# Sums of weights in the buffer of their quarters, a third raw tile, and second-half attention pieces at double distances

## The chip, the cores and the metric

One core of a Trainium2 chip runs the whole program: a two-layer decoder trunk in float32. Its engines are TensorE (PE, matmuls; PEld is its weight load), VectorE (DVE), ScalarE (ACT), GpSimd (POOL) and SyncE (SP), which issues most DMAs. Each engine works through its own list of instructions in order; semaphores order the engines among one another. The metric is the device time of one execution in microseconds (us); lower is better.

## The reference

x is 256 tokens by 2048 channels, d_ff is 8192. Each of the two layers computes

```python
h = rmsnorm(x, attn_norm_g[l])
q, k, v, gate_b, gate_c, conv_in = split(h @ w_in[l])          # six parts of 1024 columns
attn = diff_attention(rmsnorm(q), rmsnorm(k), v, lam, rel_bias)  # 8 heads, two softmaxes each
attn = rmsnorm(attn, subln_g[l]) * (1 - lam_init)
conv = gate_b * short_conv(gate_c * conv_in, conv_w[l])
x = x + concat([attn, conv]) @ w_out[l]
hm = rmsnorm(x, mlp_norm_g[l]) @ w_up[l]
x = x + square(relu(hm)) @ w_down[l]
```

## The kernel before

**Two parts of every operand.** A float32 matrix product is made of three matmuls with operands split in a high part (ACT copies and rounds it) and a low part (DVE subtracts the high part from the original). The three terms are high by high, high activation by low weight, low activation by high weight, in this order. So each weight tile costs DMA, one ACT instruction and one DVE instruction before PE can use it; `whi`, `wlo`, `uhi`, `ulo` and the parts named below are such tiles. Weights come from HBM once; the tiles `raw` (512 KB), `uraw` and `draw` (1 MB each) hold them as they arrive.

**What sets the order.** PE's instructions stand in the order in which the program writes them. Those of the other engines are placed at build time by a scheduler which plans with the dependencies and its own costs; instructions handed to `late` keep their program order. `Background.tick()`, called from the matmul loops, advances generators: a generator that yields n goes on n ticks later. So attention's pieces lie between the projection matmuls.

**Mixer.** Per layer the projections run in the order q, k, v for heads 0 to 3, q, k, v for heads 4 to 7, then (gate_C, conv_in) four times, gate_B four times, and the output projection `o`. `linear_t` makes the gate and convolution parts (`gc`, `ci`, `gb`, line 408), each with four "turned" raw tiles. `attention(..., pace)` is started twice per layer, with pace 1 for the first four heads and pace 2 for the last four. It takes four `unit`s (heads), each with scores (`sc`, line 604), softmax, then after a yield the transposes (`ptp`, line 635) and their parts `pT` (637, 638), after another yield the product with v (`av`, line 648), and after the last head the normalised `an` (668), a yield, and the transposes into `cat` (682). `staggered` starts the units a given number of ticks apart. The MLP's tiles take the room of the mixer's once these are read; the first four `uraw` loads (line 809) wait for that. SP issues them in its order among the mixer's raw loads (line 343).

**MLP.** The hidden units come in 32 pairs of blocks (index i). For each i PE makes two columns of hm (`upw`, `upc`, line 949, from `uhi`/`ulo`), ACT and DVE square them (`h`), make the four sums of activations S1 to S4, and split them into `f` (981 high, 982 low). Two pairs later (LAG = 2) the product of `f` with rows of w_down follows for the first half of w_down's columns, in a seven-product scheme instead of eight block products: product 1 takes the quarter b11 of the 2 x 2 blocks of weights, 2 takes b21, 3 takes b22, 5 and 7 take the sums t1 and t3, 6 and 4 take t2 and t4. In the MLP's first stage the products 1, 2, 3, 5 run between the two columns of pair i, the products 7, 6, 4 after the second. The second half of w_down's columns follows after the first stage: blocks `ordinary` (eight products, line 1074), and for the nine pairs in `SEVEN = (2, 4, 7, 9, 12, 14, 17, 19, 22)` the seven-product scheme in one run of 21 matmuls in the order 1, 2, 3, 5, 7, 6, 4. The activations of these pairs come back from HBM (`fb`, `back`).

**The weights of the scheme.** `quarters(i, col)` makes them in three steps. `plain` loads a `draw` tile (line 826; pool `dpool`, two buffers) and makes the parts of b11 (`b1h`, `b1l`, 512 elements per partition) and of b21, b22 (`b2h`, `b2l`, 1024 elements). `sums` makes t1, t3 in a tile `t` of 8 KB per partition (line 853, 1024 elements), their parts `t13h`, `t13l`, and then t2 (856) and t4 (857), 512 elements each. `more` makes the parts `t24h`, `t24l` of t2 and t4. All parts come from the helper lines 839 (ACT) and 840 (DVE). The `t13` and `t24` parts have one buffer each, `b1` and `b2` two.

Of the kernel before, what the change touches and what calls it, by code (L numbers as in the profile page):

```python
# [9 lines left out]
F32 = mybir.dt.float32  # L10
# [5 lines left out]
P = 128  # L16
# [12 lines left out]
CH = 512  # L29
# [59 lines left out]
def staggered(pieces, apart):  # L89

    entries = [[i * apart, p] for i, p in enumerate(pieces)]
    while entries:
        for e in list(entries):
            if e[0] <= 0:
                try:
                    e[0] = max(1, next(e[1]))
                except StopIteration:
                    entries.remove(e)
                    continue
            e[0] -= 1  # L100
        if entries:
            yield 1
# [3 lines left out]
def trunk(ctx: ExitStack, tc: tile.TileContext, x, w_in, w_out, conv_w, q_norm_g, k_norm_g,  # L106
          lambda_q1, lambda_k1, lambda_q2, lambda_k2, subln_g, attn_norm_g, mlp_norm_g,
          w_up, w_down, rel_bias, selector, out):
    nc = tc.nc
# [16 lines left out]
    def bank(name):  # L126
        return ps.tile([P, CH], F32, tag="bank", name=name)
# [456 lines left out]
    def attention(l, qT, kT, kL, v, h0, dst, bias, tmp, pace):  # L584
# [3 lines left out]
        parts = dst.open()  # L588
# [5 lines left out]
        def unit(i):  # L594
            h = h0 + i
# [30 lines left out]
            for t in range(NT):  # L626
# [2 lines left out]
                                               nlam[:, l:l + 1], op0=ALU.mult, op1=ALU.mult)  # L629
                nc.vector.scalar_tensor_tensor(p[:, w], s[:, 1, w], c[:, t:t + 1], s[:, 0, w],  # L630
                                               op0=ALU.mult, op1=ALU.add)
            yield 10
            tp = bank(f"ptp{h}")
            for b in range(3):
                nc.tensor.transpose(tp[:, b * P:(b + 1) * P], p[:, b * P:(b + 1) * P], ident)
            pT = tmp.tile([P, 2, 3 * P], F32R, tag="pT", name=f"pT{h}", bufs=1)
            nc.scalar.activation(pT[:, 0], tp[:, :3 * P], AF.Copy)
            nc.vector.tensor_sub(pT[:, 1], tp[:, :3 * P], pT[:, 0].bitcast(F32))
            yield 4

            av = ps.tile([P, CH], F32, tag="av", name=f"av{h}", bufs=1)
            av = av.rearrange("p (t n c) -> p t n c", t=NT, n=2)
# [23 lines left out]
            for t in range(NT):  # L666
# [3 lines left out]
                    ao[:, t].rearrange("p (g d) -> p g d", d=P),  # L670
                    f2[:, :, t:t + 1].to_broadcast([P, 4, P]), op=ALU.mult)
                an_.append(an)
            yield 12 if pace == 1 else 18
            for t in range(NT):
                tp = bank(f"atp{h0}_{t}")
                for b in range(4):
# [7 lines left out]
                    op0=ALU.mult, op1=ALU.subtract)  # L684
                yield 2

        yield from staggered([unit(i) for i in range(4)], 8)
        dst.ready = True

    def conv(l, q, u, cv, norm):  # L690
# [25 lines left out]
    def mixer(l, norm, loads):  # L716

        with ExitStack() as scope:
# [28 lines left out]
            for half in range(2):  # L747
                h0 = 4 * half
                acc = linear(f"q{l}{half}", hT, weights)
                r = norm.r  # L750
                qT = bpool.tile([P, 2, 4, S], F32R, tag="b", name=f"qT{l}{half}")
                work.start(qk_norm(acc, r, q_parts(qT), q_gain[:, l:l + 1], f"q{l}{half}"))
                acc = linear(f"k{l}{half}", hT, weights)
                kT = bpool.tile([P, 2, 4, S], F32R, tag="b", name=f"kT{l}{half}")
                work.start(qk_norm(acc, r, k_parts(kT, kL), k_gain[:, l:l + 1], f"k{l}{half}"))
                acc = linear(f"v{l}{half}", hT, weights)
                v = bpool.tile([P, 2, NT, CH], F32R, tag="b", name=f"v{l}{half}")
                for t in range(NT):
                    nc.scalar.activation(v[:, 0, t], acc[:, t], AF.Copy, scale=r[:, t:t + 1])
                    nc.vector.scalar_tensor_tensor(v[:, 1, t], acc[:, t], r[:, t:t + 1],  # L760
                                                   v[:, 0, t].bitcast(F32),
                                                   op0=ALU.mult, op1=ALU.subtract)
                work.start(attention(l, qT, kT, kL, v, h0, cat[half], bias, tmp,
                                     1 + half), 3 + 6 * half)
# [25 lines left out]
    def mlp(l, mnorm, last):  # L790
# [3 lines left out]
        with ExitStack() as scope:  # L794
            upool = scope.enter_context(tc.tile_pool(name="upool", bufs=4))
            fpool = scope.enter_context(tc.tile_pool(name="fpool", bufs=2))
            dpool = scope.enter_context(tc.tile_pool(name="dpool", bufs=2))
            spool = scope.enter_context(tc.tile_pool(name="spool", bufs=1))
            work.start(mnorm.factors(), 1)

# [2 lines left out]
            raws, forms = {}, {}  # L803
# [20 lines left out]
            def load_rows(i, col, pool=dpool, tag="draw"):  # L824
                raw = pool.tile([P, 2, 2 * CH], F32, tag=tag, name=tag)
                nc.sync.dma_start(
                    raw, w_down[l][i * 2 * P:(i + 1) * 2 * P, col:col + 2 * CH].rearrange(
                        "(k p) c -> p k c", p=P))
                return raw

            def quarters(i, col=0):


                keep = late if i == 0 or (i == SEVEN[0] and col) else lambda ins: None

                def parts(src, tag, bufs):
                    hi = spool.tile(list(src.shape), F32R, tag=f"{tag}h", name=f"{tag}h", bufs=bufs)
                    lo = spool.tile(list(src.shape), F32R, tag=f"{tag}l", name=f"{tag}l", bufs=bufs)
                    keep(nc.scalar.activation(hi, src, AF.Copy))  # L839
                    keep(nc.vector.tensor_sub(lo, src, hi.bitcast(F32)))  # L840
                    return hi, lo

                def plain():
                    raw = forms["raw"] = load_rows(i, col).rearrange("p k (n c) -> p k n c", n=2)
                    h1, l1 = parts(raw[:, 0, 0], "b1", 2)
                    h2, l2 = parts(raw[:, 1], "b2", 2)
                    return (h1, l1), (h2[:, 0], l2[:, 0]), (h2[:, 1], l2[:, 1])

                def sums():
                    raw = forms["raw"]  # L850
                    t = forms["t"] = spool.tile([P, 4, CH], F32, tag="t", name="t")

                    keep(nc.vector.tensor_sub(t[:, 0:2], raw[:, :, 1], raw[:, 0]))  # L853
                    h, lw = parts(t[:, 0:2], "t13", 1)

                    keep(nc.vector.tensor_add(t[:, 2], t[:, 1], raw[:, 0, 0]))
                    keep(nc.vector.tensor_sub(t[:, 3], raw[:, 1, 0], t[:, 2]))
                    return (h[:, 0], lw[:, 0]), (h[:, 1], lw[:, 1])

                def more():  # L860
                    h, lw = parts(forms["t"][:, 2:4], "t24", 1)
                    return (h[:, 0], lw[:, 0]), (h[:, 1], lw[:, 1])

                if (i, col) == (0, 0):
                    made = {}
                    forms["plain"] = lambda: made.update(p=plain())
                    forms["sums"] = lambda: made.update(s=sums())
                    return lambda: made["p"], lambda: made["s"], more
                return plain, sums, more

            def rows(i, k, box, col=0, *where):
# [124 lines left out]
            for i in range(NP):  # L996
                j = i - LAG
                end = i == NP - 1
                h = fpool.tile([P, 8, P], F32, tag="h", name="h", bufs=1)
# [12 lines left out]
                for c in range(2):  # L1012
# [24 lines left out]
                    elif j >= 0:  # L1037
                        t2, t4 = weights.take()
# [113 lines left out]
            for i in range(2 * BLK):  # L1152
# [14 lines left out]
                t2, t4 = weights.take()  # L1167
# [40 lines left out]
    for l in range(DEPTH):  # L1208
        mnorm = mixer(l, norm, first_loads if l == 0 else lambda weights: None)
        norm = mlp(l, mnorm, l == DEPTH - 1)  # L1210
# [31 lines left out]
```

## Time and profile before

| | |
|---|---|
| median of 3 runs | 2151.07 us (2148.47 to 2151.32) |
| the profiled execution | 2151.32 us, span 2149.5 us |
| PE busy | 2134.0 us (99%), 10934 matmuls |
| DVE busy | 1678.6 us (78%) |
| ACT busy | 1308.2 us (61%) |
| POOL busy | 169.8 us (8%) |
| HBM | 440.52 MB read, 33.58 MB written, 221 GB/s over the span |
| granted PE clock | 1.00 |

Times of single instructions are counted from the start of the span. A row of the timeline gives start, duration, engine, line, operation, tiles and shape; in brackets stands how long the engine was idle before, and what ended that. Where a row stands for several instructions it carries their number (x8) and the time from the first one's start to the last one's end. Neighbouring matmuls, ACT and DVE instructions overlap a little, so the distance between starts is shorter than a duration.

### The profile page before, as it was taken

The page shows a single profiled execution, that of the slowest core. Times are in us where ns is not written, and L with a number is a line of the kernel's source. Part 1 is how long each engine was busy: PE and PEld are TensorE (multiplying, and loading weights), DVE is VectorE, ACT ScalarE, POOL GpSimd, SP SyncE. Part 2 cuts the span into 40 slices and gives each one's busy share as a digit, 9 for nine tenths or more (in the row PEclk, how much of TensorE's full clock was granted, in tenths as well). Part 3 has the DMA queues.
Part 4 walks back from the last instruction along what each step waited for, and adds up shares of the span by engine and source line. Part 5 has one row for each costly group of instructions (what it writes and reads, how often), then busy time and mean ns, then how long its engine had stood idle before and what let it go on. Part 6 is the DMA issues. An engine that isn't in the chain of part 4 may idle for free. (4 is left out here: it accounts for less than half of the span.)

```text
span 2149.5 us, 28983 instructions
## 1 busy us (share of the span) xinstructions
PE 2134.0 (99%) x10934; PEld 1819.9 (85%) x10934; DVE 1678.6 (78%) x2297; ACT 1308.2 (61%) x1767; POOL 169.8 (8%) x226
## 2 busy tenths in 40 slices
PE   9999999999999999999999999999999999999999
PEld 8888888888888888888888888888888888888887
DVE  6777655799889888798566776557888888888984
ACT  6666445666666666565566654446666666665652
POOL 3111100000000000011110111000000000001110
PEclk9999999999999999999999999999999999999999
DMA  8555766577777777798665566656777777777984
GB/s 271 179 160 171 246 186 187 190 244 230 233 232 231 229 227 234 241 318 288 210 178 176 166 197 215 187 176 204 241 233 223 240 229 226 235 225 262 335 264 137
DMA packets 298524, 475.98 MB, mean 221 GB/s; under 512 B 10803, under 2 KB 191621, under 8 KB 298384
## 3 DMA queue, kind: packets, MB, share of 16 engines
q1 hardware_dynamic: 268768, 406.88, 60.4%
q0 software_dynamic: 29568, 67.24, 9.4%
q8 instruction: 85, 1.39, 0.3%
q14 instruction: 55, 0.45, 0.1%
q10 hardware_dynamic: 48, 0.02, 0.0%
HBM read 440.52 MB, written 33.58 MB: 221 GB/s over the span
## 5 line engine op out<-in xcount | busy, mean ns | idle before, releaser
L303 DVE TENSOR_TENSOR wlo<-raw,whi 128x1024 fp32r<-128x1024 f32 x286 | 352.2, 1234 | 252.3 <-ACT whi L302 245.8
L302 ACT ACTIVATE whi<-raw 128x1024 fp32r<-128x1024 f32 x286 | 303.1, 1060 | 341.1 <-PE o L386 73.6
L949 PE MATMUL upc<-nT,uhi 128*128 128x512 f32 x1920 | 477.7, 391 | 0.6 <-ACT ev L959 0.6
L816 ACT ACTIVATE uhi<-uraw 128x1024 fp32r<-128x1024 f32 x256 | 271.2, 1060 | 280.3 <-PE upc L949 260.4
L949 PEld LDWEIGHTS upc<-nT,uhi 128*128 128x128 f32 x1920 | 352.7, 188 | 69.2 <-ACT ev L959 1.1
L817 DVE TENSOR_TENSOR ulo<-uraw,uhi 128x1024 fp32r<-128x1024 f32 x256 | 312.9, 1223 | 109.3 <-ACT uhi L816 105.3
L949 PEld LDWEIGHTS upc<-nT,ulo 128*128 128x128 f32 x1920 | 261.9, 190 | 18.7
L949 PE MATMUL upc<-nT,ulo 128*128 128x256 f32 x1920 | 267.7, 282 | 0.0
L386 PE MATMUL o<-whi,cat 128*128 128x512 f32 x512 | 159.5, 390 | 0.0
L1074 PE MATMUL dn<-whi,fb 128*128 128x512 f32 x480 | 151.1, 389 | 0.0
L386 PEld LDWEIGHTS o<-whi,cat 128*128 128x128 f32 x512 | 96.1, 188 | 19.7
L302 ACT ACTIVATE whi<-uraw 128x1024 fp32r<-128x1024 f32 x60 | 63.7, 1061 | 75.7 <-PE dn L1074 70.7
L1074 PEld LDWEIGHTS dn<-whi,fb 128*128 128x128 f32 x480 | 90.1, 188 | 18.7
L386 PE MATMUL o<-wlo,cat 128*128 128x512 f32 x256 | 99.6, 389 | 0.0
L840 DVE TENSOR_TENSOR t13l<-t,t13h 128x1024 fp32r<-128x1024 f32 x78 | 95.5, 1224 | 4.0 <-ACT t13h L839 2.2
L839 ACT ACTIVATE b2h<-draw 128x1024 fp32r<-128x1024 f32 x78 | 82.5, 1058 | 24.9 <-PE pr L992 22.2
L840 DVE TENSOR_TENSOR b2l<-draw,b2h 128x1024 fp32r<-128x1024 f32 x78 | 95.5, 1224 | 2.1 <-ACT b2h L839 2.1
L840 DVE TENSOR_TENSOR t24l<-t,t24h 128x1024 fp32r<-128x1024 f32 x78 | 95.2, 1221 | 1.4 <-ACT t24h L839 0.3
L853 DVE TENSOR_TENSOR t<-draw 128x1024 f32<-128x1024 f32 x78 | 95.3, 1221 | 0.4
L992 PE MATMUL pr<-t13h,f 128*128 128x512 f32 x240 | 93.8, 391 | 0.0
L1074 PE MATMUL dn<-wlo,fb 128*128 128x512 f32 x240 | 93.4, 389 | 0.0
L303 DVE TENSOR_TENSOR wlo<-uraw,whi 128x1024 fp32r<-128x1024 f32 x60 | 73.2, 1224 | 21.1 <-ACT whi L302 20.9
(408 smaller groups left out, 4138.6 us busy)
## 6 DMA issues: line engine op xcount, KB each, us to landing
uraw<-in_w_up_dram SPq DMA_DIRECT2D x128, 1024.0 KB, 6.5
raw<-in_w_in_dram SPq DMA_DIRECT2D x191, 512.0 KB, 4.0
draw<-in_w_down_dram SPq DMA_DIRECT2D x82, 1024.0 KB, 5.3
raw<-in_w_out_dram SPq DMA_DIRECT2D x64, 512.0 KB, 3.6
uraw<-in_w_down_dram SPq DMA_DIRECT2D x30, 1024.0 KB, 6.3
raw<-in_w_down_dram SPq DMA_DIRECT2D x16, 1024.0 KB, 5.2
hid0p<-f POOLq DMA_DIRECT2D x21, 512.0 KB, 6.4
fb<-hid0p POOLq DMA_DIRECT2D x21, 512.0 KB, 5.9
```

What stands on the lines that cost most here:

```text
L302: pair = (nc.scalar.activation(hi, raw, AF.Copy), nc.vector.tensor_sub(lo, raw, hi.bitcast(F32)))
L303: nc.vector.tensor_sub(lo, raw, hi.bitcast(F32)))
L386: nc.tensor.matmul(acc[:, t], a.ap[:, pa, k % KG, t * P:(t + 1) * P], (hi, lo)[pw][:, j], start=(k == 0 and n == 0), stop=(k == nk - 1 and ...
L816: pair = (nc.scalar.activation(hi, src, AF.Copy), nc.vector.tensor_sub(lo, src, hi.bitcast(F32)))
L817: nc.vector.tensor_sub(lo, src, hi.bitcast(F32)))
L839: keep(nc.scalar.activation(hi, src, AF.Copy))
L840: keep(nc.vector.tensor_sub(lo, src, hi.bitcast(F32)))
L853: keep(nc.vector.tensor_sub(t[:, 0:2], raw[:, :, 1], raw[:, 0]))
L949: nc.tensor.matmul(acc[:, 0] if part else acc, wt[:, k], a.ap[:, 0, k % KG] if part else a.ap[:, :, k % KG], start=(part == 0 and kh == 0 ...
L992: nc.tensor.matmul(prods[n], f[:, pa, a], b[pw], start=(start and m == 0), stop=(stop and m == 2))
L1074: nc.tensor.matmul(prods[p], f[:, pa, 2 * k + t], b[pw][:, n], start=(p in starts and k == 0 and m == 0), stop=(stop and k == 1 and m == 2))
```

## The change

It has two parts. In `attention` every distance is multiplied by `pace`: the first four heads keep theirs (10, 4, 12 ticks and 8 between units), the last four get 20, 8, 24 and 16 instead of 10, 4, 18 and 8.

In `quarters` the tile `t` goes away. The sums are written over the quarters they are made of: t3 over b22 and t1 over b12 (in this order, by reversed views, since t3 reads b12 too), t2 over b11 and t4 over b21. `dpool` gets a third buffer of 8 KB per partition, which is the room that `t` had. The first sum therefore follows the `b1` and `b2` parts of the same tile, and a `draw` tile is free for the next load after its `t24l` instead of after its t4. The number of instructions on each engine and their shapes stay the same; lines behind the sums move down by two (853 becomes 854, 856 becomes 858, 857 becomes 859, 982 becomes 984, 1074 becomes 1076).

```diff
-            yield 10
+            yield 10 * pace
...
-            yield 4
+            yield 4 * pace
...
-            yield 12 if pace == 1 else 18
+            yield 12 * pace
...
-        yield from staggered([unit(i) for i in range(4)], 8)
+        yield from staggered([unit(i) for i in range(4)], 8 * pace)
...
-            dpool = scope.enter_context(tc.tile_pool(name="dpool", bufs=2))
+            dpool = scope.enter_context(tc.tile_pool(name="dpool", bufs=3))
...
                 def sums():
                     raw = forms["raw"]
-                    t = forms["t"] = spool.tile([P, 4, CH], F32, tag="t", name="t")
-                    keep(nc.vector.tensor_sub(t[:, 0:2], raw[:, :, 1], raw[:, 0]))
-                    h, lw = parts(t[:, 0:2], "t13", 1)
-                    keep(nc.vector.tensor_add(t[:, 2], t[:, 1], raw[:, 0, 0]))
-                    keep(nc.vector.tensor_sub(t[:, 3], raw[:, 1, 0], t[:, 2]))
+                    t31 = raw[:, ::-1, 1]
+                    keep(nc.vector.tensor_sub(t31, t31, raw[:, 0, ::-1]))
+                    h, lw = parts(raw[:, :, 1], "t13", 1)
+                    t2, t4 = raw[:, 0, 0], raw[:, 1, 0]
+                    keep(nc.vector.tensor_add(t2, raw[:, 1, 1], t2))
+                    keep(nc.vector.tensor_sub(t4, t4, t2))
                     return (h[:, 0], lw[:, 0]), (h[:, 1], lw[:, 1])
 
                 def more():
-                    h, lw = parts(forms["t"][:, 2:4], "t24", 1)
+                    h, lw = parts(forms["raw"][:, :, 0], "t24", 1)
                     return (h[:, 0], lw[:, 0]), (h[:, 1], lw[:, 1])
```

## The prediction

> **What bounds the kernel now.** I read the page's busy times first, then PE's waits, then the timeline around each of these, and last the order in which the changed kernel's instructions stand on each engine.
>
> ```profile
> PE 2134.0 (99%) x10934; PEld 1819.9 (85%) x10934; DVE 1678.6 (78%) x2297; ACT 1308.2 (61%) x1767; POOL 169.8 (8%) x226
> ```
> ```profile
> PE pr L992 <- DVE f L982: 3.1, 2, 1.7
> PE ci L408 <- ACT whi L302: 1.9, 2, 1.6
> PE ptp L635 <- DVE s L630: 1.7, 2, 0.8
> PE sc L604 <- DVE cat L682: 1.2, 2, 0.6
> PE warm L160 <- DVE mhalf L152: 1.1, 1, 1.1
> PE av L648 <- DVE pT L638: 1.0, 2, 0.5
> PE upc L949 <- ACT ev L959: 0.6, 1, 0.6
> ```
>
> PE is the bound: 2134.0 of 2149.5 us, and no matmul is added or removed. The second view gives us in total, times and the longest for all that PE waited for: 10.6 us, about one of each per layer. So at most about 10 us (0.5%) can be gained, and the loss is open: the sums are made anyway, but where they stand on DVE and ACT decides whether PE waits. The profiled execution took 2151.32 us (1.8 around the span), 0.25 above the median; sums are made against it. No change that this kernel's measurement can tell is 0.2%, or 4.3 us.
>
> **1. Second-half attention at double distances: -4.6.** By the changed kernel's order, `sc` stays where it is (1.2 stay). `ptp` of each later head comes 20 ticks after its scores and `av` 8 ticks after `ptp`, twice as far; ten and four more ticks of projection matmuls then cover what was late by 0.5 to 0.8 us. So 1.7 and 1.0 go. `ci` waited for a raw tile:
>
> ```profile
> 1206.83 66.08 SPq L343 DMA_DIRECT2D raw<-in_w_in_dram  x20
> 1273.99 7.39 SPq L809 DMA_DIRECT2D uraw<-in_w_up_dram  x4
> 1281.48 13.30 SPq L343 DMA_DIRECT2D raw<-in_w_in_dram  x5
> ```
> ```profile
> 1292.08 1.06 ACT L302 ACTIVATE whi<-raw 128x1024 fp32r<-128x1024 f32 x1 [7.80 <-DMA raw<-in_w_in_dram]
> ```
>
> SP stood at the four `uraw` loads until attention's last tiles were free, issued 4 MB in a row, and the next raw tile came behind them: 1292.08 - 1273.99 = 18.1 us for 4.5 MB. The changed order has three `uraw`, one raw, the fourth `uraw`, ten raw tiles later than before, when the tiles are long free. Three `uraw` and a raw take 3.5/4.5 of 18.1 = 14.1 us, and ACT could do with 18.1 - 1.6 = 16.5; the raw behind the fourth has 5 MB before it lands, 20.1 us against 16.5 and one raw tile's distance (66.08/20 = 3.3), 19.8. So `ci`'s 1.9 go, with 0 to 0.3 per layer given back; I take 0. Sum: 1.7 + 1.0 + 1.9 = 4.6. The cover of the remaining waits is PE's projection work, which is the same.
>
> **2. A third raw tile removes the stall late in the product stage: -3.7.** In layer 1:
>
> ```profile
> 1507.24 10.11 SPq L809 DMA_DIRECT2D uraw<-in_w_up_dram  x2
> 1517.59 0.40 SPq L826 DMA_DIRECT2D draw<-in_w_down_dram  x1
> ```
> ```profile
> 1528.79 0.63 ACT L839 ACTIVATE b1h<-draw 128x512 fp32r<-128x512 f32 x1 [5.29 <-DMA draw<-in_w_down_dram]
> 1533.32 2.11 PE L949 MATMUL upc<-nT,uhi 128*128 128x512 f32 x8 [0.65 <-ACT ev L959]
> 1541.29 0.50 PE L992 MATMUL pr<-b1h,f 128*128 128x512 f32 x1 [1.66 <-DVE f L982]
> ```
>
> With two tiles the load waited for t4 of two pairs back, went out behind two `uraw` loads, and ACT could use it 11.2 us after its issue; ACT stood 5.29 us with `ev`, `f` and all else queued behind `b1h`. After, three loads go out at the stage's start and each later one waits for `t24l` of three pairs back, a whole pair earlier than needed. So PE's 3.1 (`pr`) and 0.6 (`upc`) go.
>
> The Trainium skill, "Perfetto Trace Analysis", section Identifying Performance Opportunities, says that the same gap repeating on the engine that should be saturated can mean too little SBUF for the next tile. The `b1h` row agrees, and by that rule alone the buffer would be a plain gain of these 3.7 us; the next two points are what it does not count.
>
> **3. The first sums of each layer stand ahead of the first product: +8.0.** Before, `f` of pair 0 was done long before the first product:
>
> ```profile
> 1484.89 1.04 ACT L981 ACTIVATE f<-h 128x1024 fp32r<-128x1024 f32 x1
> 1489.52 1.06 ACT L816 ACTIVATE uhi<-uraw 128x1024 fp32r<-128x1024 f32 x1
> ```
> ```profile
> 1486.16 1.22 DVE L982 TENSOR_TENSOR f<-h,f 128x1024 fp32r<-128x1024 f32 x1
> 1490.24 1.22 DVE L840 TENSOR_TENSOR t13l<-t,t13h 128x1024 fp32r<-128x1024 f32 x1
> ```
> ```profile
> 1490.27 0.40 PE L992 MATMUL pr<-b1h,f 128*128 128x512 f32 x1
> 1492.34 0.39 PE L992 MATMUL pr<-t13h,f 128*128 128x512 f32 x1
> ```
>
> In the changed order pair 1's sums stand among the `ulo` of pairs 1 and 2, and `f` of pair 0 comes after the `uhi` of 1489.52, which waits for PE's room and can't be earlier. So on ACT `f` follows at 1490.5 to 1491.5; on DVE, after that `ulo`, at 1491.8 to 1493.0. Product 1's first matmul starts at 1491.6 instead of 1490.27 (+1.3), its third needs the low part and starts at 1493.0 (+1.0). Pair 0's t1, t3 come after `f` on DVE, to 1494.1; ACT's `t13h` then ends at 1495.2, and product 5, due at 1494.6, starts 0.6 late; `t13l` ends at 1496.5, 1.1 late for the second matmul. 1.3 + 1.0 + 0.6 + 1.1 = 4.0 per layer; layer 0 has the same order. Laid out further, `f` of the next pairs is some 4 us ahead. Bounds: the wait for `f` alone (2.3), up to 5 if DVE picks up small work in between; twice that, 4.6 to 10.
>
> **4. The first seven-product group of the second half: +19.6.** This is the largest term. Before:
>
> ```profile
> 1983.38 1.22 DVE L840 TENSOR_TENSOR t13l<-t,t13h 128x1024 fp32r<-128x1024 f32 x1
> 1988.07 1.23 DVE L840 TENSOR_TENSOR t24l<-t,t24h 128x1024 fp32r<-128x1024 f32 x1
> 1991.81 1.23 DVE L303 TENSOR_TENSOR wlo<-uraw,whi 128x1024 fp32r<-128x1024 f32 x1 [0.24 <-ACT whi L302]
> 1993.55 0.69 DVE L840 TENSOR_TENSOR b1l<-draw,b1h 128x512 fp32r<-128x512 f32 x1
> 1994.16 1.22 DVE L840 TENSOR_TENSOR b2l<-draw,b2h 128x1024 fp32r<-128x1024 f32 x1
> 1995.29 0.69 DVE L840 TENSOR_TENSOR b1l<-draw,b1h 128x512 fp32r<-128x512 f32 x1
> ```
> ```profile
> 1990.71 1.06 ACT L302 ACTIVATE whi<-uraw 128x1024 fp32r<-128x1024 f32 x1 [1.67 <-PE dn L1074]
> 1991.68 0.61 ACT L839 ACTIVATE b1h<-draw 128x512 fp32r<-128x512 f32 x1
> ```
> ```profile
> 1998.62 0.39 PE L992 MATMUL pr1r<-b1h,fb 128*128 128x512 f32 x1
> 2000.88 0.39 PE L992 MATMUL pr1r<-t13l,fb 128*128 128x512 f32 x1
> 2002.02 0.39 PE L992 MATMUL pr1r<-t24h,fb 128*128 128x512 f32 x1
> 2002.24 0.39 PE L992 MATMUL pr1r<-t24l,fb 128*128 128x512 f32 x1
> ```
>
> Pair 2's sums were ready 10 to 17 us before the group, ahead of `b1h`, which stands behind a `whi` that waits for PE until 1990.71. In place they can only follow `b1`, `b2`. The changed kernel's DVE order from 1991.81 is: `wlo`, b1l and b2l of pairs 2 and 4, t31 of 2, `wlo`, t31 of 4, `fb`, `wlo`, **t13l of 2**, t2 of 2, `wlo`, t2 of 4, b1l and b2l of 7, **t4 of 2**, t4 of 4, t13l of 4, t31 of 7, **t24l of 2**. Consecutive starts above are 1.13 apart for 1024 elements (1994.16 to 1995.29) and 0.61 for 512 (1993.55 to 1994.16). In place the sums have the same shapes; I take the same prices. Then:
> - t13l of 2 is the ninth 1024 after two 512s: it ends at about 2003.3. Product 5's second matmul (2000.88) waits 2.5.
> - t4 of 2 comes after two more 1024s and five more 512s in all, ends near 2008.0; ACT's `t24h` (1.06) ends at 2009.1. Product 6, due at 2002.02 + 2.5, waits 4.6. ACT can't save it: pair 4's `t13h` stands before it and waits for product 7.
> - t24l of 2 is the fourteenth 1024 with seven 512s: 1991.8 + 20.1, end 2012.0. Product 6's second matmul waits another 2.7.
>
> Together 9.8 per layer, twice: 19.6. DVE has no gap in this stretch, so nothing hides it. Lower bound: without any DVE backlog pair 4's `t13h`, `t24h` and then `t13l`, t31, `t24l` still stand in order behind product 7, two ACT steps and three DVE steps less one overlap, about 4.6 per layer. Upper bound: 12, with one wait for a `uraw` more. The groups that follow have their loads and sums a group ahead, as before; I count 0.
>
> **Sum:** 2151.3 - 4.6 - 3.7 + 8.0 + 19.6 = 2170.6; against the median 0.25 less. I say **2170**.
>
> **Rivals.**
> - *The backlog is shorter than laid out* (DVE's prices less, the order's small instructions elsewhere): part 4 costs 4.6 to 6.3 per layer. -8.3 + 8.0 + 9.2 to 12.6: 2160 to 2164. For it: DVE's idle share is 22% on average; against: it has no gap here. 0.17.
> - *The waits cost PE its clock.* The trace shows what a slow start costs:
>
> ```profile
> 1.05 5.06 PE L160 MATMUL warm<-ones 128*128 128x128 f32 x22 [1.05 <-DVE mhalf L152]
> ```
> ```profile
> 6.78 0.83 PE L160 MATMUL warm<-ones 128*128 128x128 f32 x6
> ```
>
> The first 22 warm-up matmuls took 0.23 us each, later ones 0.14. If part 4's wait of 4.6 us puts PE back in that state, the next 5 us run at about half speed: +2.5 per layer, 2175 to 2176. No wait in this trace is long enough to show it; the matmul after the longest, 1.66 us, took 0.50 against 0.40 at 1490.27. The Trainium skill, "TensorE: Matmul & The Clock Gate", section Why this matters for your kernels, states that an idle gap of over about 3 us returns PE to half clock; the trace of before has no such gap. 0.09.
> - *Only the gains arrive.* If `f` at the first product and the sums of pair 2 come in time, that is because DVE works off its backlog ahead of the group, the time is 2151.3 - 8.3 = 2143, faster. It decides at the `t13l` of pair 2: were it done by 2000.9 and `t24l` by 2002.2, 10 us earlier than laid out, nothing is lost. For it speaks that the mean DVE load is 78%; against it the fixed order on each engine. 0.07.
> - *The gains and part 3 alone* (part 4 hidden): 2151. 0.05.
> - *The third tile brings nothing*, since the late load stood behind two `uraw` loads whatever released it: 2174. 0.04, against it the three loads at the stage's start.
>
> **How the numbers follow.** The forecast as laid out has 0.58, from 2166 to 2174. Faster by over 0.2% is the gains-only case and part of the fifth's lower edge: 0.08. Within 0.2%: 0.06. Slower: 0.86. The range 2158 to 2176 takes in the forecast, the short backlog, and the clock's case; about 0.15 lies outside.
>
> **What would show it.** In the changed profile PE's waits should list `pr` on `f` in both layers (about 1.3 and 1.0 at the first product), and the `pr1r` rows of the first group on t13l, t24h and t24l with about 2.5, 4.6 and 2.7. `ci`, `ptp` and `av` should be gone from PE's waits, `sc` stay. PE's busy time stays near 2134 if the clock holds. The forecast is wrong if the first group of seven runs through without a wait, if DVE shows idle time between 1992 and 2012, or if a `ci` wait is still there.

## The result and the profile after

The changed kernel takes 2174.29 us (median, 2172.59 to 2174.36) against 2151.2 (four runs of each): ratio 1.0106, 95% interval 1.009 to 1.0122, so some 23 us slower. The profiled execution has a span of 2172.5 us against 2149.5. First the page's busy times and PE's waits of the changed kernel (us in total, times, longest):

```profile
PE 2145.3 (99%) x10934; PEld 1827.0 (84%) x10934; DVE 1700.3 (78%) x2297; ACT 1324.7 (61%) x1767; POOL 165.4 (8%) x226
```
```profile
PE pr1r L994 <- ACT t24h L839: 3.8, 1, 3.8
PE pr0r L994 <- ACT t24h L839: 3.3, 1, 3.3
PE pr L994 <- issue: 2.4, 2, 1.2
PE pr1r L994 <- DVE t13l L840: 2.3, 1, 2.3
PE pr0r L994 <- DVE t13l L840: 2.3, 1, 2.3
PE pr0r L994 <- DVE t24l L840: 2.1, 1, 2.1
PE pr1r L994 <- DVE t24l L840: 2.1, 1, 2.1
PE pr L994 <- DVE f L984: 1.4, 2, 0.7
PE sc L604 <- DVE cat L682: 1.2, 2, 0.6
PE warm L160 <- DVE mhalf L152: 1.1, 1, 1.1
PE pr L994 <- DVE t13l L840: 0.5, 1, 0.5
```

`ci`, `ptp`, `av` and the `upc` wait are gone, `sc` is the same. New are the waits of the first seven-product group (its products go to the tiles pr0r in layer 0 and pr1r in layer 1: 15.9 us in both layers) and those at the first product (2.4 + 1.4 + 0.5). The waits went from 10.6 to 22.5 us. But PE is also busy for 11.3 us longer with the same matmuls. The timeline of layer 1 shows both, DVE first, then PE:

```profile
2003.21 0.68 DVE L840 TENSOR_TENSOR b1l<-draw,b1h 128x512 fp32r<-128x512 f32 x1
...
2012.36 1.22 DVE L840 TENSOR_TENSOR t13l<-draw,t13h 128x1024 fp32r<-128x1024 f32 x1
...
2021.05 1.22 DVE L840 TENSOR_TENSOR t24l<-draw,t24h 128x1024 fp32r<-128x1024 f32 x1
```
```profile
2013.63 0.50 PE L994 MATMUL pr1r<-t13l,fb 128*128 128x512 f32 x1 [2.27 <-DVE t13l L840]
...
2019.40 0.80 PE L994 MATMUL pr1r<-t24h,fb 128*128 128x512 f32 x1 [3.82 <-ACT t24h L839]
2022.32 0.80 PE L994 MATMUL pr1r<-t24l,fb 128*128 128x512 f32 x1 [2.12 <-DVE t24l L840]
...
2024.62 0.63 PE L1076 MATMUL dn<-whi,fb 128*128 128x512 f32 x1
```

A matmul that took 0.39 us takes 0.63. The windows view (PE, PEld, DVE, ACT, POOL busy, then the granted clock) tells why:

```profile
2000.00:2010.00 10.00, 10.00 (x46) 8.29 (x45) 8.51 (x9) 8.73 (x10) 0.60 (x1) 1.00 0.83 291
2010.00:2014.00 4.00, 1.73 (x9) 1.11 (x8) 4.00 (x5) 1.82 (x3) 0.67 (x2) 1.00 0.73 199
2014.00:2028.00 14.00, 8.06 (x19) 5.51 (x18) 10.78 (x13) 3.17 (x3) 0.70 (x1) 0.51 0.57 203
```

After the first waits the granted clock drops: it is 0.5 from 2014.3 to 2028.0, for 13.7 us, and as long in layer 0 (that waits do this, and what it costs, is tested below). At the first product it happened too, for one stretch of 3.41 us in layer 1 and two in layer 0:

```profile
1498.89:1502.31 3.42, 1.53 (x10) 0.92 (x9) 2.43 (x3) 2.38 (x3) 0.00 (x0) 1.00 1.06 367
1502.31:1505.72 3.41, 3.41 (x8) 2.46 (x8) 3.32 (x5) 2.13 (x4) 0.76 (x1) 0.50 0.79 267
```

Why the first product came late shows in the timelines of ACT and PE:

```profile
1498.79 1.06 ACT L816 ACTIVATE uhi<-uraw 128x1024 fp32r<-128x1024 f32 x1 [1.73 <-PE upc L951]
1499.75 1.04 ACT L983 ACTIVATE f<-h 128x1024 fp32r<-128x1024 f32 x1
```
```profile
1500.89 0.47 PE L994 MATMUL pr<-b1h,f 128*128 128x512 f32 x1 [1.19 <-issue]
```

The high part of pair 0's `f` stands behind a `uhi` for which ACT waits for PE, and ends at 1500.79, just before the product starts. The profile puts this wait of 1.19 us down to "issue"; by these times it is a wait for `f`.

### The profile page after: what moved, and what is told of

Read it like the earlier page. It is cut to its first block, busy times and chain, and to the rows that moved or that the text cites. A ratio compares the mean times of both kernels' runs of the same rounds, so it can differ in the third digit from the quotient of the medians.

```text
span 2172.5 us, 28857 instructions
## 1 busy us (share of the span) xinstructions
PE 2145.3 (99%) x10934; PEld 1827.0 (84%) x10934; DVE 1700.3 (78%) x2297; ACT 1324.7 (61%) x1767; POOL 165.4 (8%) x226
## 4 chain that ended last, share of the span: by engine, by line
PE 96%; DVE 2%; ACT 1%; issue 0%; DVEq 0%; ACTq 0%
PE upc L951 31%; PE pr L994 13%; PE o L386 8%; PE dn L1076 7%; PE ci L408 4%; PE gb L408 4%; PE k L386 4%; PE q L386 4%; PE v L386 4%; PE dn L1145 4%; PE gc L408 4%; PE dn L994 2%; PE pr1r L994 1%; PE pr0r L994 1%; PE upw L951 1%; PE up L951 1%
## 5 line engine op out<-in xcount | busy, mean ns | idle before, releaser
L303 DVE TENSOR_TENSOR wlo<-raw,whi 128x1024 fp32r<-128x1024 f32 x286 | 356.6, 1248 | 234.9 <-ACT whi L302 230.3
L839 ACT ACTIVATE t24h<-draw 128x1024 fp32r<-128x1024 f32 x78 | 82.9, 1063 | 33.9 <-PE pr L994 16.1
L840 DVE TENSOR_TENSOR t24l<-draw,t24h 128x1024 fp32r<-128x1024 f32 x78 | 95.3, 1222 | 9.5 <-ACT t24h L839 8.8
L840 DVE TENSOR_TENSOR t13l<-draw,t13h 128x1024 fp32r<-128x1024 f32 x78 | 95.3, 1222 | 5.5 <-ACT t13h L839 2.2
L854 DVE TENSOR_TENSOR draw<-draw 128x1024 f32<-128x1024 f32 x78 | 95.4, 1222 | 1.6
```

What stands on the lines that cost most here:

```text
L303: nc.vector.tensor_sub(lo, raw, hi.bitcast(F32)))
L854: keep(nc.vector.tensor_sub(t31, t31, raw[:, 0, ::-1]))
```

## The experiments

The theory is the prediction's: doubled distances gain, sums in place lose by where they stand on DVE and ACT. The rivals: DVE has no room for them anywhere; the third tile brings nothing; the slow clock only fills time in which PE would have waited. Ratios are to the kernel before on the same chip, with 95% intervals in brackets; where two ratios are subtracted, the interval given combines both.

**Doubled distances alone.** The four `pace` lines of the diff on the kernel before.

> The kernel before with the doubled distances of second-half attention alone. Theory (prediction, part 1): ptp, av and ci disappear from PE's waits, sc stays with 1.2, the time falls by 4.6 us to about 2146.6. Rival: the raw tile behind the fourth uraw load comes late and ci keeps 0.3 to 0.8 us per layer: 2147.2 to 2148.2. Rival: the second half's pieces only push other work, no change: 2151.

Measured: 2144.16 us, ratio 0.996 (0.9945 to 0.9975). It was run again beside later kernels:

> The kernel before with the doubled distances alone once more, on the same chip as the ordered one: 2144. If the third tile is worth its part of the prediction, the ordered kernel is 2 to 4 us below it; if not, both agree within 1 us.

Measured: 2144.58 us, ratio 0.9967 (0.9955 to 0.998): faster by 7.1 us (4.3 to 9.7). The ordered kernel (below) took 2150.45 us on the same chip, 5.9 us more, so neither of the two cases expected here came. The waits of the second run:

```profile
PE pr L992 <- DVE f L982: 3.3, 2, 1.6
PE sc L604 <- DVE cat L682: 1.2, 2, 0.6
...
PE ci L408 <- ACT whi L302: 0.5, 1, 0.5
```

What was to go has gone, but for 0.5 of `ci` in one run of two. The gain is larger than the 4.6 of the list. Adding up the distances between successive starts on PE in the traces of before and of the first run, the steps into matmuls of `ci`, `ptp`, `av` and `gc` became shorter by 3.1, 2.3, 1.1 and 0.8 us, 7.3 together, where the list has 1.9, 1.7, 1.0 and nothing. The list counts from the modelled end of the matmul before, and the start-up behind a wait (0.50 us for a matmul of 0.40) is not in it. How much each of the two takes was not separated.

**Sums in place alone.** The changed kernel with the old distances.

> The changed kernel with the old distances in second-half attention: third tile and sums in place alone. Theory, the two parts add up: 2174.3 + 4.6 = 2178.9 us, with the waits on f, t13l, t24h, t24l of the changed kernel in both layers and ptp, av, ci as before. Rival, the two parts interact (the attention part moves loads that the product stage needs): under 2176 or over 2182.

Measured: 2180.98 us, ratio 1.0136 (1.0119 to 1.0153). The parts add up: 1.0136 - 1.0106 is 0.3%, the gain of the distances.

**Pair 2's pin taken away.**

```diff
-                keep = late if i == 0 or (i == SEVEN[0] and col) else lambda ins: None
+                keep = late if i == 0 else lambda ins: None
```

> The changed kernel without the pin that holds pair 2's instructions of the second half in program order on ACT and DVE; the scheduler may now place its b1, b2 and sums earlier. Theory (the wait is one of order, not of room on DVE): the pr0r and pr1r waits of 7.7 and 8.2 us go, and with them the half clock after the last of them (4.9 and 5.6 us at half speed, 5.2 lost): 2174.3 - 15.9 - 5.2 = 2153. Rival (DVE has no room for the sums at all before the group): waits of 4.6 per layer stay, about 2162 to 2165. Rival (another pair takes its place and waits): no gain, 2174.

Measured: 2167.43 us, ratio 1.0068 (1.0053 to 1.0083). The pr0r and pr1r waits are gone, and waits for `f` took their place:

```profile
PE pr L1076 <- DVE f L984: 9.1, 2, 4.6
PE pr L1076 <- ACT f L983: 3.9, 2, 1.9
```

The scheduler put pair 2's `b1` and `b2` of the second half, among other work, ahead of the last `f` of the first half. No expectation gave this time (2153, 2162 to 2165, 2174). The second rival held as to the mechanism, that another product waits instead, but some 7 to 8 us were gained all the same. There is room on DVE, but where it is taken decides who waits.

**Pair 2 brought forward, by hand.** Its parts and sums of the second half keep their pin, but are written into the program earlier, ahead of the two column blocks:

```diff
-                if (i, col) == (0, 0):
-                    made = {}
-                    forms["plain"] = lambda: made.update(p=plain())
-                    forms["sums"] = lambda: made.update(s=sums())
+                if (i, col) == (0, 0) or col and i == SEVEN[0]:
+                    made, again = {}, "again" if col else ""
+                    forms["plain" + again] = lambda: made.update(p=plain())
+                    forms["sums" + again] = lambda: made.update(s=sums())
...
+            forms["plainagain"]()
+            forms["sumsagain"]()
             for n in range(2):
                 columns(lambda k, pa, t: fs[NP - LAG + k // 2][:, pa, k % 2 * 2 + t], n, start=True)
```

> The changed kernel with pair 2's parts and sums of the second half brought forward, the first product's order as changed. It takes part 4 away alone. Theory (predicted 19.6, and 20.5 between the kernels with pair 1 pinned): 2174.3 - 20 = about 2154, with the 1.19 + 0.70 + 0.5 us of waits at the first product and their two to four stretches of half clock left. Rival (part 4's cost is partly taken up by a later wait): 2160 or more.

Measured: 2150.87 us, ratio 0.9997 (0.9988 to 1.0006). This takes part 4 away alone: 1.0106 - 0.9997 is 1.09%, 23.4 us (19 to 27). Its waits:

```profile
PE pr L994 <- issue: 2.4, 2, 1.2
PE dn L1145 <- DVE wlo L303: 1.6, 2, 0.8
PE pr L994 <- DVE f L984: 1.4, 2, 0.7
...
PE pr L994 <- DVE t13l L840: 0.8, 1, 0.8
PE pr L994 <- ACT t13h L839: 0.3, 1, 0.3
```

No pr0r or pr1r; a wait of 1.6 us at the column blocks is new, a cost of bringing the work forward. Against the doubled distances alone 0.9997 - 0.9967 = 0.3% is left, 6.5 us (3 to 10). Less the new 1.6, that leaves about 5 us for parts 2 and 3 together; no run separates them.

**Pair 1 held back.** Two ways were tried to mend the order at the first product. First a pin for pair 1 as for pair 0:

```diff
-                keep = late if i == 0 or (i == SEVEN[0] and col) else lambda ins: None
+                keep = late if i <= 1 and not col or (i == SEVEN[0] and col) else lambda ins: None
```

> The changed kernel with pair 1's instructions of the first half pinned in program order like pair 0's, so that its sums no longer stand ahead of pair 0's f; the second half as changed. Theory (prediction, part 3): PE's waits on f, t13h and t13l at the first product go in both layers and the clock stays at 1.00 there; against the pace-alone kernel the changed one spends 4.0 us more in the up matmuls and 5 more in pr once the late load's 3.5 are set off, so 2174.3 - 9 = about 2165 to 2167. Rival (pair 1's parts now come too late for its own products): the waits move by one pair, 2172 or more.

Measured: 2183.49 us, ratio 1.0144 (1.0129 to 1.016); the rival held. Pair 1's own products now wait for its t13 parts:

```profile
PE pr L994 <- DVE t13l L840: 7.5, 2, 3.9
PE pr L994 <- ACT t13h L839: 5.1, 2, 2.5
```

With pair 2 brought forward as well:

> As the one before, and pair 2's parts and sums of the second half are written into the program ahead of the two column blocks that follow the first half, so that ACT and DVE make them there. Theory: both new costs of the sums in place are gone, doubled distances and third tile keep their gains: 2144.2 (doubled distances alone) less the 3.5 us that PE waits on f and ev behind the late load: 2140.7, clock 1.00. Rival (what is brought forward delays the parts of those column blocks, as f was delayed where the pin was left out): 2145 to 2155. Rival (a third tile is worth nothing once the order is right): 2144.

Measured: 2163.02 us, ratio 1.0052 (1.0039 to 1.0065): the pr0r and pr1r waits are gone here too, which is worth 20.5 us between these two. Pair 1's waits stay (12.6 us), so the time lies above the theory and both rivals. The second way is an order without a pin: pair 1's first sum goes behind pair 0's `t24l` on DVE, as it stands in the kernel before.

```diff
+    def behind(ins, prev):
+        tc.add_manual_dep(ins.ins, prev.ins.name, mybir.DependencyInfo(
+            mybir.DependencyClass.NoSync, mybir.DependencyReason.DATA), reason="behind")
...
+                    if (i, col, tag) == (0, 0, "t24"):
+                        forms["last"] = ins
...
+                    if (i, col) == (1, 0):
+                        behind(ins, forms["last"])
```

> The changed kernel with both orders mended: pair 1's first sum is issued behind pair 0's t24l on DVE (an order, no wait), and pair 2's parts and sums of the second half are written into the program ahead of the two column blocks. On the engines f, t13 and t24 of pair 0 then stand as in the kernel before. Theory (part 3 is a matter of order alone): no wait on f, t13h or t13l at the first product, no pr0r or pr1r wait, clock 1.00, doubled distances and third tile keep their gains: 2140 to 2143, faster than both. Rival (the sums in place are too late for some product in any order): a wait of 2 us or more per layer is left, 2147 or more.

Measured: 2150.45 us, ratio 0.9994 (0.9985 to 1.0003), the same as with pair 2 brought forward alone. The theory failed here, and the rival's 2 us or more per layer came: pair 0's waits are gone, and pair 1's `f` is late instead, behind a `uhi` for which ACT waits for PE. Waits first, then ACT's timeline (lines of this kernel stand 10 further on):

```profile
PE pr L1004 <- DVE f L994: 2.3, 2, 1.2
PE pr L1004 <- ACT f L993: 2.3, 2, 1.1
```
```profile
1501.78 1.06 ACT L820 ACTIVATE uhi<-uraw 128x1024 fp32r<-128x1024 f32 x1 [1.73 <-PE upc L961]
1502.74 1.04 ACT L993 ACTIVATE f<-h 128x1024 fp32r<-128x1024 f32 x1
```

It is the mechanism of part 3, one pair later. Whether any order of these sums is free of it stays open: of the three that were run (as changed, pinned, ordered), each has such a wait.

**Two tiles instead of three.** The last kernel with `bufs=2` for `dpool`.

> The ordered kernel with two raw tiles instead of three. Theory (the third tile is what removes the late load; sums in place hold a tile longer, until t24l): loads go out later than in the kernel before, ACT waits on draw and PE on f or ev by more than the 3.7 us of before: 2146 to 2155. Rival (the order alone removes the wait): as the ordered kernel.

Measured: 2196.49 us, ratio 1.0207 (1.0191 to 1.0222). That is 46 us more than with three, much more than expected, and not once but all along the stage. PE waits for `ev`, and ACT waits for `draw` tiles at `b1h`, with `ev` and all else queued behind it:

```profile
PE upc L961 <- ACT ev L971: 34.6, 31, 2.0
```
```profile
ACT b1h L843 <- DMA draw<-in_w_down_dram: 122.5, 49, 3.8
```

With three tiles the first of these waits is 0.3 us in all and the second 1.1, once each. With sums in place the third tile is thus not a gain but a need: it pays for holding a tile until `t24l`. The Trainium skill, "Perfetto Trace Analysis", section Identifying Performance Opportunities, says that a gap repeating on the engine that should be saturated can mean too little room for the next tile; these 31 waits of PE agree. The `b1h` row that the prediction set beside this sentence was a single gap on ACT, so it was weak support. What a third tile is worth with the sums in a tile of their own was not run.

**The clock by itself.** The changed kernel with small matmuls ahead of the products that wait, into banks which these start anew:

```diff
+            def fill(n, bank_):
+                for _ in range(n):
+                    nc.tensor.matmul(bank_[:, :P], ones, ones, start=True, stop=True)
...
+                        if j == 0:
+                            fill(10, prods[1])
                         product(1, f, A11, b11, j == 0, end)
...
+                    if start and n in (5, 6):
+                        fill({5: 18, 6: 52}[n], prods[n])
```

> The changed kernel with 10 small filler matmuls ahead of the first product of each layer, and 18 and 52 ahead of products 5 and 6 of the first group of the second half, written to banks that the next product starts anew, so that PE is not idle while it waits; results unchanged. Theory (the granted clock is a cost of its own): the clock stays at 1.00, the waits shrink by the fillers, and the matmuls behind the last waits run at full speed: 4.3 + 4.9 + 3.4 + 5.6 us at half speed cost 9.1, of which later waits hid some 2, so the time falls by 5 to 9 us to 2165 to 2169. Rival (the slow clock only fills time in which PE would have waited): 2174, within 1 us. Rival (the fillers themselves delay PE): 2175 or more.

Measured: 2180.53 us, ratio 1.0128 (1.0113 to 1.0143), clock 1.00. I had taken a filler for one matmul of 0.11 us; in the trace it is two (20 matmuls in 2.39 us for 10 fillers), so the fillers were longer than the waits. With half as many (5, 9, 26):

> As the kernel with fillers, with half as many (5 ahead of the first product, 9 and 26 ahead of products 5 and 6): a filler turned out to be two matmuls of 0.11 us, so the first try filled 17.9 us per layer, more than PE waits. Theory (the granted clock is a cost of its own): clock 1.00, no wait longer than before, 2165 to 2169. Rival (the slow clock only fills time in which PE would have waited): 2174.

Measured: 2169.28 us, ratio 1.0079 (1.0065 to 1.0093), clock 1.00. The last wait of the first seven-product group of layer 1 is still there:

```profile
2019.61 0.50 PE L994 MATMUL pr1r<-t24l,fb 128*128 128x512 f32 x1 [1.23 <-DVE t24l L840]
```

This matmul starts 13.39 us after the first of its group (2006.22), as in the changed kernel (2022.32 - 2008.93 = 13.39). The fillers shortened nothing up to there: so far the slow clock had only filled waiting time. But behind this matmul nothing waits: the next 30 starts take 9.57 us in the changed kernel and 6.94 with fillers, in layer 0 9.23 and 6.93. So the half clock costs 2.6 and 2.3 us there. The measured difference agrees: the kernel with fillers is 0.27%, 5.8 us (1.2 to 10.4), faster than the changed one. So of the 23 us some 5 to 6 are the slow clock, and the rival "it only fills time" falls for the matmuls behind the last wait.

**Which gap halves it.** The kernel before with 19 gaps made by chains of additions on DVE, one ahead of each projection but the first.

> The kernel before with 19 gaps made on purpose: ahead of each projection of q, k, v and out (but the very first) PE waits for a chain of 1 to 7 additions on DVE of about 0.6 us each, which nothing else uses. It measures what gap halves the granted clock. Theory (the clock is set for each stretch of 3.41 us by the idle share of the one before, about half of it): gaps up to 1.5 us never halve it, those of 1.7 to 3.4 do depending on where they fall, those over 3.4 always, and half clock lasts whole stretches. Rival (only a gap of over 3 us does it): of the gaps under 3 us none. The time is longer by the gaps, some 50 us, and by the slow stretches.

Measured: 2369.05 us. The gaps came out longer than meant (up to 14.6 us, since the chains stood behind other work on DVE), but enough short ones are there. The records of the clock change only at multiples of 3.41 us from one another. One of the waits (lines of this kernel stand 16 further on), and the windows view cut at these points around three of them, of 1.66, 2.01 and 2.82 us (PE busy is the first number after the length):

```profile
1478.79 2.62 PE L424 MATMUL ci<-nT,whi 128*128 128x512 f32 x8 [2.01 <-ACT whi L302]
```
```profile
572.25:575.66 3.41, 1.75 (x13) 1.28 (x11) 3.41 (x4) 1.55 (x2) 0.00 (x0) 1.00 1.02 345
575.66:579.00 3.34, 3.34 (x15) 2.72 (x16) 3.34 (x6) 2.12 (x3) 0.67 (x1) 1.00 1.08 354
```
```profile
1476.78:1480.19 3.41, 1.40 (x7) 1.18 (x7) 1.32 (x2) 2.25 (x3) 0.00 (x0) 1.00 0.68 235
1480.19:1483.61 3.42, 3.42 (x14) 3.02 (x13) 3.27 (x4) 2.36 (x3) 1.61 (x1) 0.50 0.64 182
```
```profile
469.85:473.26 3.41, 1.49 (x8) 1.27 (x9) 1.86 (x3) 0.52 (x2) 0.00 (x0) 1.00 0.51 160
473.26:476.67 3.41, 3.41 (x11) 2.66 (x10) 0.00 (x0) 0.16 (x1) 0.00 (x0) 0.50 0.30 106
```

A stretch with 49% idle kept the clock, those with 59% and 56% (the third) lost it for the next. The theory holds but for two stretches of 56 and 57% that did not halve it; both were the beginning of a longer gap, and the stretch after them did. The rival (only over 3 us) falls with the 2.01 us wait.

## Why the prediction was right, and where it was off

The forecast was 2170 with a range of 2158 to 2176; 2174.3 lies within, 4 us over the forecast. What was measured is the forecast's mechanism together with the clock's rival, which had 0.09 and gave 2175 to 2176. That the total is so near has some luck in it: part 1 gained some 2.5 us more than forecast, and the half clock, at nothing in the forecast, cost some 5 to 6.

- **Part 1** said -4.6; it is -7.1 (-9.7 to -4.3). The waits named are those that went. What was off is to read the gain as the sum of the listed waits; they are too short as prices.
- **Parts 2 and 3** said -3.7 and +8.0, +4.3 together; measured is +6.5 with the 1.6 of the column blocks, about 5 without. The late load's waits did go. At the first product 1.3 and 1.0 were foreseen; 1.2 and 0.7 are listed, 1.4 and 0.9 from start to start. Of the 0.6 and 1.1 for t13, 0.5 is listed in layer 0 and nothing in layer 1. There PE ran at half clock and came later, which had been foreseen only for a wait of 4.6 us. Where the clock stayed at 1.00 at this place, in layer 1 of the kernel with pair 2 brought forward, both waits are listed, with 0.3 and 0.8.
- **Part 4** said 2.5, 4.6, 2.7 and +19.6. Listed are 2.3, 3.8 (3.3 in layer 0) and 2.1, and taking the part away gained 23.4, with the new 1.6 some 25. From start to start the three delays are 2.4, 4.6 and 2.7 against the kernel before, 9.8 per layer, just what was forecast; the listed waits are shorter because PE came to them later at half clock. The rest is the half clock behind the last wait, 2.6 and 2.3 us, for which the clock's rival had said 2.5. DVE's order and prices were as laid out: from b1l of pair 2 (2003.21) to the start of t24l (2021.05) it had no gap. One count in the text was wrong, four more 512s and not five up to t4, without effect on its sum.
- **The short backlog** falls: DVE had none to spare here. **Only the gains** falls as to the whole, though the gains are there. **The third tile brings nothing** falls: the waits behind the late load went with it, and the kernel with two tiles is 46 us slower.

The fastest version is the kernel before with the doubled distances alone, 2144.6 us.

## What to carry over

Writing a result over its operands saves a buffer and adds an order: all readers of the operand must now come first, and on engines that run in order a pin or a planner may put them much later than the data would allow. Before trading a buffer for such an order, lay out the engine's queue at the first use after each change of stage; in this kernel both new costs arose there. And price a wait on PE twice, by its length and by the clock behind it: what counts is how long PE runs at half clock after the last wait.

## What the hardware showed

The granted clock goes by stretches of 3.41 us. Over the 14 traces here, a stretch at full clock in which PE was idle for over 60% halved the clock for the next in every case, with 50 to 60% in 13 of 15, with 48 to 49% in one of four (layer 0 of the changed kernel), and with less never; the ends of matmuls are modelled, so the shares are a little rough. The clock came back after a stretch with at most 8% idle and after none with 15% or more. So a wait of 2.0 us can be enough if it falls within one stretch, or 1.2 and 0.7 us close together. The Trainium skill, "TensorE: Matmul & The Clock Gate", gives a window of 3.4 us in its section What's actually happening, and the stretches here agree. The same page of the Trainium skill, section Why this matters for your kernels, warns of idle gaps of PE over about 3 us; here less was enough, and the measurement decides.
